# LayerNorm in four blocks of 258 tokens, and the second pointwise convolution by column groups and token quarters

## The chip, the cores and the metric

The kernel runs on one core of a Trainium2 chip. Five engines work side by side: TensorE (PE in the profile; its weight loads are PEld), VectorE (DVE), ScalarE (ACT), GpSimd (POOL) and SyncE (SP), whose queue issues most of the DMAs. Each engine executes its own instructions in order and waits for the others at semaphores. The metric is the device time of one execution in microseconds; lower is better.

## The reference

One inference step of a two-layer trunk over 1024 prompt tokens and 8 decode tokens (T = 1032 columns in the kernel, 1024 features as 8 tiles of 128 partitions). Layer 0 mixes tokens with a Conformer convolution module, layer 1 with a Mamba-2 mixer; each layer then has a SwiGLU feed-forward and a gated per-layer embedding. The change lies in layer 0:

```python
def conformer_mixer(u, buf, w_pw1, b_pw1, w_dw, b_dw, ln_g, ln_b, w_pw2, b_pw2):
    a = u @ w_pw1 + b_pw1
    v = jax.nn.glu(a, axis=-1)
    c, new_buf = causal_dwconv(v, buf, w_dw, b_dw)
    c = jax.nn.silu(layernorm(c, ln_g, ln_b))
    return c @ w_pw2 + b_pw2, new_buf

h = h + o                                          # o is the mixer's result
h = h + swiglu(rmsnorm(h, g_ffn[i]), ...)
```

The layernorm's mean and variance run over the 1024 features of one token, so over the partitions of all 8 tiles.

## The kernel before, in words

Tokens lie along the free dimension. Every big product is done in three passes of a split operand (`mm3`: high times high, high times low, low times high), so each operand, weight or activation, is first split: a copy rounded to the short form (`split`, on ACT, line 110) and the remainder by a subtraction (line 111, on DVE). One 128 x 1024 weight tile is loaded by SP into `wraw` (two buffers) and split into `whi` and `wlo` (`slab`, line 124). One group of the second pointwise convolution (`product`) is 24 matmuls, 8 feature tiles times 3 passes, into one of 7 PSUM banks.

The order of the work around the change:

1. The depthwise convolution ends with `h[m]` (8 tiles of 128 x 1032) and their sum `cs`, which DVE adds up in the three blocks of `BLK` (344 tokens each).
2. While that goes on, PE has filler work: 12 steps of `ple_products` (the projection of the per-layer embeddings, line 240 evicts them), handed out by `FILL` at fixed places of the program.
3. LayerNorm in three blocks of 344 tokens. `center` subtracts the mean (a matmul of `cs` with a constant matrix, line 726; the subtraction, line 732, is on DVE). `square` sums squares into a statistics tile: in block 0 the squares are on ACT (line 194) and the sums on DVE (line 195), in blocks 1 and 2 both are on POOL (lines 186, 188, 195). `finish` is a matmul (line 204), a square root on ACT (line 209, with a table load), a reciprocal on DVE (line 210), and a one-element Silu that brings back the other table (line 742). `apply` multiplies by the reciprocal root (DVE, line 748), does Silu with scale and bias (ACT, line 750), and makes both parts of the split on DVE (lines 751 and 752).
4. After all three blocks `hp.close()` gives up the memory of `h`, and an `Entry` takes it. Only then are the residual's pieces of `x` loaded into its tiles `ha` and `hb` (line 786). `h` here means both halves of 516 tokens, `j` = 0 and 1.
5. The second pointwise convolution for `j`, for `m`, for two quarters `b` of 258 tokens: product, eviction with bias and residual (DVE, line 794), then `Entry.add`: a store to `h_d` in DRAM (line 270), the square (ACT, lines 275 and 278) and its sum (POOL, line 279). All 8 weight tiles are loaded and split twice, once for each half.
6. After `m` = 1 of half 1, `entry.finish(0)` and `entry.prepare(0)`: the RMSNorm of half 0 (line 285 is its matmul), and the operands of the feed-forward (`b1`, `b2`, `t2`, seven split operands). `gate_up` follows with half 0 first, and makes `finish(1)` and `prepare(1)` after its first weights.

The program is written in this order, and a scheduler orders the instructions of each engine by it and by when it expects operands; the SP queue is one of the queues that it orders. Tiles that take memory from a closed pool wait for the last use of each tile that lay there.

Of the kernel before, what the change touches and what calls it, by code (L numbers as in the profile page):

```python
# [16 lines left out]
P = 128  # L17
# [10 lines left out]
BLK = ((0, 344), (344, 344), (688, 344))  # L28
BLKP = ((0, 388), (388, 386), (774, 258))
# [28 lines left out]
def trunk_kernel(ctx: ExitStack, tc: tile.TileContext, I, O):  # L58
# [28 lines left out]
    V.memset(warm, 1.0)  # L87
    half = const.tile([P, 4], F32, name="half")
# [160 lines left out]
    class Entry:  # L249
# [15 lines left out]
        def add(self, j, m, b):  # L265
# [5 lines left out]
            if self.acc[j] is None:  # L271
                self.acc[j] = self.np.tile([P, HT], F32, name="acc", tag="acc")
                self.rstd[j] = self.np.tile([P, HT], F32, name="rstd", tag="rstd", bufs=2)
            if m == 0:
                S.activation(out=self.acc[j][:, o:o + QT], in_=x, func=AF.Square)
                return
            sq = self.np.tile([P, QT], F32, name="sq", tag="sq", bufs=2)
            S.activation(out=sq, in_=x, func=AF.Square)
            G.tensor_tensor(out=self.acc[j][:, o:o + QT], in0=self.acc[j][:, o:o + QT], in1=sq, op=ALU.add)

        def finish(self, j):
            for b in range(2):
# [256 lines left out]
    with tc.tile_pool(name="l0", bufs=2, reuse_waits="tile") as pool:  # L539
# [50 lines left out]
        with tc.tile_pool(name="conv", bufs=2, reuse_waits="tile") as cp:  # L590
# [24 lines left out]
            def conv(m, v):  # L615
# [14 lines left out]
                elif m == KT - 1:  # L630
                    for o, n in BLK:
                        V.tensor_tensor(out=cs[:, o:o + n], in0=cs[:, o:o + n], in1=c[:, o:o + n], op=ALU.add)
                else:
                    V.tensor_tensor(out=cs, in0=cs, in1=c, op=ALU.add)
# [47 lines left out]

            vs = []
# [19 lines left out]
            for m in range(KT):  # L703
# [4 lines left out]
                if m == KT - 1:  # L708
# [4 lines left out]
                    it = chain(ple_products(cp, ps, 1, U[6:], "v"), ple_products(cp, ps, 0, U[4:6], "v", (1,)))  # L713
# [5 lines left out]

            ln = Norm(ps)  # L720
            for _ in range(FILL[1]):
                next(it)
            mus = []
            for o, n in BLK:
                mu = ps.tile([P, 512], F32, name="mu", tag="mm")
                TE.matmul(mu[:, :n], lhsT=mean, rhs=cs[:, o:o + n], start=True, stop=True)
                mus.append(mu)

            def center(b, m):
                o, n = BLK[b]  # L730
                cx = h[m][:, o:o + n]
                return V.tensor_tensor(out=cx, in0=cx, in1=mus[b][:, :n], op=ALU.subtract)

            def square(b, m):
                o, n = BLK[b]
                return ln.add(h[m][:, o:o + n], o, n, V if b == 0 else G, None if b == 0 else G)

            def finish(b, root_behind=(), recip_behind=()):
                root, recip = ln.finish(*BLK[b])
                behind(root, *root_behind)  # L740
                behind(recip, *recip_behind)
                behind(S.activation(out=warm[:, :1], in_=warm[:, 1:], func=AF.Silu), root)
                return root, recip

            def apply(b, m):
                o, n = BLK[b]
                t = npool[0].tile([P, 384], F32, name="un", tag="un", bufs=2)
                x = V.tensor_tensor(out=t[:, :n], in0=h[m][:, o:o + n], in1=ln.rstd[:, o:o + n], op=ALU.mult)
                s = pool.tile([P, 384], F32, name="s", tag="s")
                y = S.activation(out=s[:, :n], in_=t[:, :n], func=AF.Silu, bias=col("ln_b", m), scale=col("ln_g", m))  # L750
                V.tensor_copy(out=U[m][0][:, o:o + n], in_=s[:, :n])  # L751
                z = V.tensor_tensor(out=U[m][1][:, o:o + n], in0=s[:, :n], in1=as32(U[m][0][:, o:o + n]), op=ALU.subtract)  # L752
                return x, y, z

            for m in range(KT):
                center(0, m)
                x = square(0, m)
            for m in range(4):
                behind(center(1, m), x)
                square(1, m)  # L760
            for _ in range(FILL[2]):
                next(it)
            root, recip = finish(0)
            for _ in it:
                pass
            for m in range(KT):
                x, y, z = apply(0, m)
            for m in range(4, KT):
                behind(center(1, m), recip)
                square(1, m)  # L770
            for m in range(KT):
                behind(center(2, m), x)
                square(2, m)
            for b in (1, 2):
                finish(b, (y,), (z,))
                for m in range(KT):
                    x, y, z = apply(b, m)
# [4 lines left out]
    for j in range(2):  # L782
        for b in range(2):
            for m in range(KT):
                o = QT * b
                nc.sync.dma_start(out=entry.h[j][m][:, o:o + QT], in_=I["x"][m, :, HT * j + o:HT * j + o + QT])
        for m in range(KT):
            w = kview(slab(I["w_pw2"][m], 1024), KT)
            for b in range(2):
                o = QT * b  # L790
                a = ps.tile([P, 512], F32, name="a", tag="mm")
                product(a[:, :QT], w, 0, U, HT * j + o, QT)
                hx = entry.h[j][m][:, o:o + QT]
                V.scalar_tensor_tensor(out=hx, in0=a[:, :QT], scalar=col("b_pw2", m), in1=hx, op0=ALU.add, op1=ALU.add)
                entry.add(j, m, b)
            if j == 1 and m == 1:
                entry.finish(0)
# [663 lines left out]
```

## Time and profile before

| | |
|---|---|
| median of 3 runs | 3101.6 us (3101.09 to 3102.29) |
| time of the profiled execution | 3103.0 us |
| its span, first to last instruction | 3101.2 us |
| mean granted TensorE clock | 0.975 of full speed |
| PE busy / DVE busy / ACT busy / POOL busy | 95% / 65% / 45% / 18% of the span |
| depthwise convolution's sum `cs` complete | 266.3 us into the span |
| last matmul of the second pointwise convolution | starts at 417.5 us |

The stage of the change is about 150 us long and lies between 265 and 418 us. Shares over the whole span say nothing about it, so the rows below are taken from windows inside it. "Busy" of a group of rows counts overlapping instructions once; the mean is that of one instruction alone, so busy divided by the count is the pitch of a back-to-back series and the mean is what one costs by itself.

### The profile page before, as it was taken

What the parts mean: (1) busy time and instruction counts of PE and PEld (TensorE: products, weight loads), DVE (VectorE), ACT (ScalarE), POOL (GpSimd) and SP (SyncE); (2) the same over time, 40 slices, a digit from 0 to 9 for tenths busy, and PEclk for the clock granted to TensorE, in tenths of its full rate; (3) what the DMA queues carried; (4) which work ended last, traced back from release to release, by engine and by line L of the source; (5) the groups of instructions that cost most, each with busy time, mean ns of one, the idle gap of its engine ahead of it and who ended that gap; (6) DMA issues with size and microseconds to landing.
All of it is one profiled execution on the core that took longest, in us unless ns stands there. A gap on an engine that the chain in (4) does not pass through costs nothing. (4 is left out here: it accounts for less than half of the span.)

```text
span 3101.2 us, 51140 instructions
## 1 busy us (share of the span) xinstructions
PE 2941.5 (95%) x20513; PEld 2893.8 (93%) x20513; DVE 2022.4 (65%) x3255; ACT 1402.5 (45%) x2470; POOL 556.8 (18%) x571
## 2 busy tenths in 40 slices
PE   9997989999999999999999999988979999989997
PEld 9997889999999999899999999888979999989997
DVE  8778695555444488467788777875595555444486
ACT  6225453333321155667667676732353333321164
POOL 0003210000000021144454444441210000000022
PEclk9998999999999999999999999998999999999998
DMA  6335522222252233122233222442422222252222
GB/s 191 75 80 179 160 88 94 76 79 73 82 185 89 65 111 102 54 87 91 92 108 106 94 92 100 144 159 79 124 77 82 81 83 83 69 179 88 65 88 87
DMA packets 146415, 313.23 MB, mean 101 GB/s; under 512 B 16513, under 2 KB 66049, under 8 KB 146177
## 3 DMA queue, kind: packets, MB, share of 16 engines
q1 hardware_dynamic: 143872, 301.51, 30.0%
q10 hardware_dynamic: 2304, 8.46, 0.7%
q8 instruction: 161, 2.64, 0.4%
q14 instruction: 78, 0.63, 0.1%
HBM read 233.15 MB, written 68.35 MB: 97 GB/s over the span
## 5 line engine op out<-in xcount | busy, mean ns | idle before, releaser
L130 PE MATMUL mm<-u,whi 128*128 128x388 f32 (+3 forms) x1472 | 481.1, 328 | 35.0 <-ACT raw L848 25.2
L131 PE MATMUL mm<-u,whi 128*128 128x388 f32 (+3 forms) x1472 | 487.3, 331 | 7.6 <-DVE u L111 7.6
L132 PE MATMUL mm<-u,wlo 128*128 128x388 f32 (+3 forms) x1472 | 477.7, 325 | 0.6 <-DVE wlo L111 0.6
L110 ACT ACTIVATE whi<-wraw 128x1024 fp32r<-128x1024 f32 (+1 forms) x199 | 207.8, 1044 | 454.4 <-PE a L131 263.7
L130 PEld LDWEIGHTS mm<-u,whi 128*128 128x128 f32 x1472 | 283.3, 193 | 39.2 <-ACT raw L848 26.6
L130 PE MATMUL a<-hh,whi 128*128 128x344 f32 x984 | 309.0, 321 | 10.9 <-ACT hh L110 10.9
L131 PE MATMUL a<-hh,whi 128*128 128x344 f32 x984 | 315.3, 321 | 0.6 <-DVE hh L111 0.6
L132 PE MATMUL a<-hh,wlo 128*128 128x344 f32 x984 | 314.5, 320 | 0.0
L195 POOL TENSOR_TENSOR stat<-stat,sq 128x344 f32<-128x344 f32 x56 | 60.0, 1072 | 1392.7 <-ACT sq L194 1390.4
L131 PEld LDWEIGHTS mm<-u,whi 128*128 128x128 f32 x1472 | 283.9, 193 | 12.4 <-DVE u L111 10.3
L132 PEld LDWEIGHTS mm<-u,wlo 128*128 128x128 f32 x1472 | 283.6, 193 | 2.5 <-DVE wlo L111 0.8
L111 DVE TENSOR_TENSOR wlo<-wraw,whi 128x1024 fp32r<-128x1024 f32 (+1 forms) x199 | 244.3, 1228 | 62.5 <-ACT whi L110 59.2
L460 DVE TENSOR_TENSOR h<-a,h 128x344 f32<-128x344 f32 x288 | 144.7, 512 | 174.9 <-PE a L132 174.1
L130 PE MATMUL a<-u,whi 128*128 128x344 f32 (+1 forms) x712 | 224.9, 317 | 15.4 <-DVE u L751 9.8
L131 PE MATMUL a<-u,whi 128*128 128x344 f32 (+1 forms) x712 | 223.2, 315 | 7.2 <-DVE u L752 7.2
L132 PE MATMUL a<-u,wlo 128*128 128x344 f32 (+1 forms) x712 | 220.9, 313 | 2.7 <-DVE wlo L111 2.7
L130 PEld LDWEIGHTS a<-hh,whi 128*128 128x128 f32 x984 | 184.4, 189 | 11.4 <-ACT hh L110 11.4
L131 PEld LDWEIGHTS a<-hh,whi 128*128 128x128 f32 x984 | 185.5, 189 | 1.0 <-DVE hh L111 1.0
L132 PEld LDWEIGHTS a<-hh,wlo 128*128 128x128 f32 x984 | 185.4, 189 | 0.0
L130 PEld LDWEIGHTS a<-u,whi 128*128 128x128 f32 x712 | 137.3, 193 | 18.3 <-DVE u L751 10.9
L111 DVE TENSOR_TENSOR wal<-sa,wah 128x1024 fp32r<-128x1024 f32 x44 | 53.9, 1224 | 151.6 <-ACT wah L110 151.6
L131 PEld LDWEIGHTS a<-u,whi 128*128 128x128 f32 x712 | 137.1, 193 | 10.0 <-DVE u L752 8.7
(361 smaller groups left out, 8652.6 us busy)
## 6 DMA issues: line engine op xcount, KB each, us to landing
wraw<-in_w_in SPq DMA_DIRECT2D x48, 512.0 KB, 3.7
hid<-hid SPq DMA_DIRECT2D x88, 258.0 KB, 2.5
hraw<-hid SPq DMA_DIRECT2D x44, 516.0 KB, 4.2
wraw<-in_w_gate SPq DMA_DIRECT2D x44, 512.0 KB, 3.2
wraw<-in_w_up SPq DMA_DIRECT2D x44, 512.0 KB, 3.3
wraw<-in_w_pw SPq DMA_DIRECT2D x32, 512.0 KB, 3.4
wraw<-in_w_down SPq DMA_DIRECT2D x32, 512.0 KB, 3.4
am<-ac_d SPq DMA_DIRECT2D x64, 256.0 KB, 3.3
```

What stands on the lines that cost most here:

```text
L110: S.activation(out=hi, in_=raw, func=AF.Copy)
L111: eng.tensor_tensor(out=lo, in0=raw, in1=as32(hi), op=ALU.subtract)
L130: TE.matmul(out, lhsT=wh, rhs=xh, start=start, stop=False, skip_group_check=onto)
L131: TE.matmul(out, lhsT=wh, rhs=xl, start=False, stop=False, skip_group_check=onto)
L132: TE.matmul(out, lhsT=wl, rhs=xh, start=False, stop=stop, skip_group_check=onto)
L195: return eng.tensor_tensor(out=self.acc[:, o:o + n], in0=self.acc[:, o:o + n], in1=sq[:, :n], op=ALU.add)
L460: V.tensor_tensor(out=h[m][:, o:o + n], in0=a[:, :n], in1=h[m][:, o:o + n], op=ALU.add)
```

## The change

- LayerNorm goes by `BLQ`, four blocks of 258 tokens, in place of three of 344. All squares are on ACT, all sums of squares on POOL. The high part of the split is an ACT copy (`split`) in place of a DVE cast.
- The second pointwise convolution of half 0 is in the LayerNorm's part of the program (`pw2_first`): after block 0 the output tiles 0 to 5 for quarter 0, after block 1 the same tiles for quarter 1, with their six split weights kept in memory, and then tiles 6 and 7 for both quarters ahead of `apply(3)`. Its residual is loaded from `x` into a small tile `rx` of its own (4 buffers), the result goes from there to `h_d` in DRAM and is squared into `acc0`, a constant tile.
- After `hp.close()` half 0 is read back from `h_d` into the `Entry`'s tiles, half 1's residual comes from `x` in whole halves (8 loads in place of 16 for each half), and half 1 is computed as before, with its 8 weight tiles loaded again.
- The convolution's pool is closed before the LayerNorm. A new pool `lnw` takes its place, with the filler's staging tiles, the small tiles and four more pairs of split weights.

```diff
+BLQ = tuple((T // 4 * b, T // 4) for b in range(4))
...
+    acc0 = const.tile([P, HT], F32, name="acc0")
...
-                self.rstd[j] = self.np.tile([P, HT], F32, name="rstd", tag="rstd", bufs=2)
+            self.square(self.acc[j][:, o:o + QT], x, m, self.np)
+
+        @staticmethod
+        def square(acc, x, m, pool):
             if m == 0:
-                S.activation(out=self.acc[j][:, o:o + QT], in_=x, func=AF.Square)
+                S.activation(out=acc, in_=x, func=AF.Square)
                 return
-            sq = self.np.tile([P, QT], F32, name="sq", tag="sq", bufs=2)
+            sq = pool.tile([P, QT], F32, name="sq", tag="sq", bufs=2)
             S.activation(out=sq, in_=x, func=AF.Square)
-            G.tensor_tensor(out=self.acc[j][:, o:o + QT], in0=self.acc[j][:, o:o + QT], in1=sq, op=ALU.add)
+            G.tensor_tensor(out=acc, in0=acc, in1=sq, op=ALU.add)

         def finish(self, j):
+            self.rstd[j] = self.np.tile([P, HT], F32, name="rstd", tag="rstd", bufs=2)
...
-                    for o, n in BLK:
+                    for o, n in BLQ:
                         V.tensor_tensor(out=cs[:, o:o + n], in0=cs[:, o:o + n], in1=c[:, o:o + n], op=ALU.add)
...
+        with tc.tile_pool(name="lnw", bufs=1, reuse_waits="tile") as lp:
+            lent.pool = lp
             ln = Norm(ps)
             for _ in range(FILL[1]):
                 next(it)
...
+            def center(b):
+                o, n = BLQ[b]
                 mu = ps.tile([P, 512], F32, name="mu", tag="mm")
                 TE.matmul(mu[:, :n], lhsT=mean, rhs=cs[:, o:o + n], start=True, stop=True)
+                for m in range(KT):
+                    cx = h[m][:, o:o + n]
+                    V.tensor_tensor(out=cx, in0=cx, in1=mu[:, :n], op=ALU.subtract)
+                    ln.add(cx, o, n, G)
+
+            def finish(b):
+                root, recip = ln.finish(*BLQ[b])
                 behind(S.activation(out=warm[:, :1], in_=warm[:, 1:], func=AF.Silu), root)
...
+            def apply(b):
+                o, n = BLQ[b]
+                for m in range(KT):
+                    t = lp.tile([P, QT], F32, name="lt", tag="lt", bufs=4)
+                    V.tensor_tensor(out=t, in0=h[m][:, o:o + n], in1=ln.rstd[:, o:o + n], op=ALU.mult)
+                    S.activation(out=t, in_=t, func=AF.Silu, bias=col("ln_b", m), scale=col("ln_g", m))
+                    split(t, U[m][0][:, o:o + n], U[m][1][:, o:o + n])
+
+            def pw2_first(m, w, b):
+
+                o, n = BLQ[b]
+                x = lp.tile([P, QT], F32, name="rx", tag="rx", bufs=4)
+                nc.sync.dma_start(out=x, in_=I["x"][m, :, o:o + n])
+                a = ps.tile([P, 512], F32, name="a", tag="mm")
+                product(a[:, :n], w, 0, U, o, n)
+                V.scalar_tensor_tensor(out=x, in0=a[:, :n], scalar=col("b_pw2", m), in1=x, op0=ALU.add, op1=ALU.add)
+                nc.sync.dma_start(out=h_d[0][m, :, o:o + n], in_=x)
+                Entry.square(acc0[:, o:o + n], x, m, lp)
+
+            def pw2_weights(m, extra):
+                return kview(slab(I["w_pw2"][m], 1024, lp if extra else None, 4), KT)
+
+            center(0)
+            for _ in range(2):
                 next(it)
+            center(1)
+            finish(0)
             for _ in it:
                 pass
+            ws = [pw2_weights(m, False) for m in range(2)]
+            apply(0)
+            for m in range(6):
+                if m >= 2:
+                    ws.append(pw2_weights(m, True))
+                pw2_first(m, ws[m], 0)
+            finish(1)
+            apply(1)
+            center(2)
+            for m in range(6):
+                pw2_first(m, ws[m], 1)
+            finish(2)
+            center(3)
+            apply(2)
+            finish(3)
+            for m in (6, 7):
+                w = pw2_weights(m, False)
+                for b in range(2):
+                    pw2_first(m, w, b)
+            apply(3)

     hp.close()
     xs = ExitStack()
     entry = Entry(0, ps, xs.enter_context(tc.tile_pool(name="xe0", bufs=1, reuse_waits="tile")))
+    entry.acc[0] = acc0
+    for m in range(KT):
+        nc.sync.dma_start(out=entry.h[0][m], in_=h_d[0][m, :, :HT])
+    for m in range(KT):
+        nc.sync.dma_start(out=entry.h[1][m], in_=I["x"][m, :, HT:])
+    for m in range(KT):
+        w = kview(slab(I["w_pw2"][m], 1024), KT)
...
```

## Rows read from the trace of the kernel before

**Rows 1.** The page's engines: busy us, share of the span, instructions.
```profile
PE 2941.5 (95%) x20513; PEld 2893.8 (93%) x20513; DVE 2022.4 (65%) x3255; ACT 1402.5 (45%) x2470; POOL 556.8 (18%) x571
```
**Rows 2.** Busy time by stage: stretch, length, engines, PE clock, DMA share, GB/s.
```profile
284.80:311.50 26.70, 9.72 (x30) 6.52 (x28) 26.56 (x40) 11.86 (x18) 20.48 (x23) 0.59 0.16 60
311.50:337.00 25.50, 21.14 (x146) 20.12 (x146) 23.57 (x49) 15.18 (x21) 0.74 (x1) 0.90 0.21 66
337.00:345.00 8.00, 6.72 (x35) 6.72 (x36) 4.00 (x9) 3.36 (x8) 2.08 (x3) 0.57 0.97 292
345.00:378.80 33.80, 33.38 (x279) 33.18 (x278) 12.16 (x17) 9.37 (x16) 10.43 (x11) 1.00 0.75 221
378.80:417.60 38.80, 36.48 (x295) 35.67 (x294) 36.64 (x40) 20.96 (x30) 12.95 (x12) 1.00 0.34 108
417.60:455.00 37.40, 30.52 (x209) 28.00 (x208) 35.55 (x44) 21.95 (x32) 2.64 (x2) 0.91 0.15 48
```
**Rows 3.** PE's waits from 284 to 418 us: total us, times, longest us.
```profile
PE a L130 <- DVE u L751: 9.8, 3, 5.0
PE a L131 <- DVE u L752: 7.2, 5, 3.4
PE a L130 <- DVE ha L794: 4.4, 1, 4.4
```
**Rows 4.** PE's timeline: start us, us, engine, line, out<-in, idle before.
```profile
279.35 0.74 PE L204 MATMUL st<-stat,mean 128*128 128x344 f32 x2
...
284.81 0.31 PE L132 MATMUL a<-u,wlo 128*128 128x344 f32 x1
...
378.96 0.60 PE L285 MATMUL st<-acc,mean 128*128 128x258 f32 x2
```
**Rows 5.** DVE's groups from 265 to 337 us: busy us, mean ns | idle before.
```profile
L748 DVE TENSOR_TENSOR un<-h,stat 128x344 f32<-128x344 f32 x24 | 16.2, 690 | 0.1
L752 DVE TENSOR_TENSOR u<-s,u 128x344 fp32r<-128x344 f32 x24 | 14.4, 605 | 0.2
L732 DVE TENSOR_TENSOR h<-h,mu 128x344 f32<-128x344 f32 x24 | 10.5, 504 | 0.1
L751 DVE CAST u<-s 128x344 fp32r<-128x344 f32 x24 | 9.9, 414 | 0.8 <-ACT s L750 0.7
```
**Rows 6.** ACT's groups from 265 to 337 us.
```profile
L750 ACT ACTIVATE s<-un,vec 128x344 f32<-128x344 f32 x24 | 16.0, 672 | 24.0 <-DVE u L752 20.0 <-DVE un L748 3.8
L240 ACT ACTIVATE pstg<-a 128x344 f32<-128x344 f32 x19 | 8.3, 456 | 4.1 <-PE a L132 4.1
L209 ACT ACT_TABLE_LOAD x3 | 3.8, 1283 | 0.4 <-ACT pstg L240 0.4
L209 ACT ACTIVATE stat<-st,eps 128x344 f32<-128x344 f32 x3 | 1.6, 549 | 0.0
```
**Rows 7.** Groups from 337 to 418 us, on DVE, ACT and POOL.
```profile
L111 DVE TENSOR_TENSOR wlo<-wraw,whi 128x1024 fp32r<-128x1024 f32 x12 | 15.7, 1309 | 8.4 <-ACT whi L110 8.0 <-DMA ha<-in_x 0.4
...
L794 DVE SCALAR_TENSOR_TENSOR ha<-a,vec,ha 128x258 f32<-128x258 f32 x16 | 7.5, 484 | 13.1 <-PE a L132 9.5 <-DMA ha<-in_x 2.9 <-DMA hb<-in_x 0.7
...
L288 DVE RECIPROCAL rstd<-rstd 128x258 f32<-128x258 f32 x2 | 3.5, 1766 | 1.0 <-ACT rstd L287 1.0
...
L110 ACT ACTIVATE whi<-wraw 128x1024 fp32r<-128x1024 f32 x12 | 12.7, 1058 | 16.8 <-PE a L131 13.6 <-DMA wraw<-in_w_pw 3.2
L278 ACT ACTIVATE sq<-ha 128x258 f32<-128x258 f32 x14 | 5.6, 413 | 10.4 <-DVE ha L794 9.2 <-POOL acc L279 1.2
...
L279 POOL TENSOR_TENSOR acc<-acc,sq 128x258 f32<-128x258 f32 x26 | 25.5, 990 | 79.2 <-ACT sq L278 66.7 <-ACT acc L275 12.5
```
**Rows 8.** The SP queue's timeline from 261 to 345 us.
```profile
263.74 70.51 SPq L124 DMA_DIRECT2D wraw<-in_w_pw  x6
334.29 7.67 SPq L786 DMA_DIRECT2D ha<-in_x  x16
```
**Rows 9.** The SP queue's waits from 265 to 420 us.
```profile
SPq L124 <- DVE wlo L111: 73.1, 8, 36.0
```

More of the change, by code (lines that the diff above doesn't have):

```diff
@@ L681, in bands, with tile @@
                 V.tensor_tensor(out=phases(c)[0], in0=phases(c)[0], in1=back, op=ALU.add)
+            class Lent:
+                pool = cp
+                def tile(self, *args, **kw):
+                    return self.pool.tile(*args, **kw)
+            lent = Lent()
             vs = []
@@ L712, in trunk_kernel @@
                     U[:4] = [(utile(0), utile(0)) for _ in range(4)]
-                    it = chain(ple_products(cp, ps, 1, U[6:], "v"), ple_products(cp, ps, 0, U[4:6], "v", (1,)))
+                    it = chain(ple_products(lent, ps, 1, U[6:], "v"), ple_products(lent, ps, 0, U[4:6], "v", (1,)))
                     for _ in range(FILL[0]):
@@ L722, in trunk_kernel @@
                 next(it)
-            mus = []
-            for o, n in BLK:
+            def center(b):
+                o, n = BLQ[b]
                 mu = ps.tile([P, 512], F32, name="mu", tag="mm")
                 TE.matmul(mu[:, :n], lhsT=mean, rhs=cs[:, o:o + n], start=True, stop=True)
[L727 to L741, printed above, removed]
-                behind(S.activation(out=warm[:, :1], in_=warm[:, 1:], func=AF.Silu), root)
[L743 to L761, printed above, removed]
+                for m in range(KT):
[4 more added lines that the diff above has]
+                root, recip = ln.finish(*BLQ[b])
+                behind(S.activation(out=warm[:, :1], in_=warm[:, 1:], func=AF.Silu), root)
@@ L762, in trunk_kernel @@
+            def pw2_weights(m, extra):
+                return kview(slab(I["w_pw2"][m], 1024, lp if extra else None, 4), KT)
+            center(0)
+            for _ in range(2):
                 next(it)
-            root, recip = finish(0)
+            center(1)
+            finish(0)
             for _ in it:
                 pass
[L766 to L777, printed above, removed]
+            ws = [pw2_weights(m, False) for m in range(2)]
[5 more added lines that the diff above has]
+            finish(1)
@@ L781, in trunk_kernel @@
     entry = Entry(0, ps, xs.enter_context(tc.tile_pool(name="xe0", bufs=1, reuse_waits="tile")))
-    for j in range(2):
-        for b in range(2):
[L784 to L797, printed above, removed]
-                entry.prepare(0)
-                entry.first.close()
+    entry.acc[0] = acc0
[5 more added lines that the diff above has]
+        w = kview(slab(I["w_pw2"][m], 1024), KT)
+        for b in range(2):
+            o = QT * b
+            a = ps.tile([P, 512], F32, name="a", tag="mm")
+            product(a[:, :QT], w, 0, U, HT + o, QT)
+            hx = entry.h[1][m][:, o:o + QT]
+            V.scalar_tensor_tensor(out=hx, in0=a[:, :QT], scalar=col("b_pw2", m), in1=hx, op0=ALU.add, op1=ALU.add)
+            entry.add(1, m, b)
+        if m == 1:
+            entry.finish(0)
+            entry.prepare(0)
+            entry.first.close()
     h, hp, U, rstd = ffn(0, entry, ps, xs)
```

## The prediction

> **What bounds the kernel now.** I read the page's engine shares first, then PE's busy time by stage, then PE's waits in the stage that the change touches, then the groups of the engines that PE waits for there, and the SP queue last. (The page's chain of waits holds only the last few microseconds of the program and says nothing here.) PE is busy 95% of the span [rows 1], so a step is worth what PE loses beside it. PE ends its filler at 284.81 + 0.31 = 285.1 us [rows 4] and works without a gap until then. In the next 26.7 us it is busy 9.7 us at a granted clock of 0.59, while DVE is busy 26.56 of 26.70 us [rows 2]: DVE sets the pace. PE's waits name it: 9.8 us for the cast and 7.2 us for the remainder of the LayerNorm's operands, the longest 5.0 us, the first wait after the filler [rows 3]. ACT waits 20.0 us for DVE in the same stage [rows 6], and DVE itself has next to no idle time in it [rows 5]. A last wait of 4.4 us is for the residual [rows 3]: SP issues it from 334.29 us on [rows 8], when the memory of `h` is given up; the 8 us after that run at a clock of 0.57 [rows 2]. From 345 us on PE is busy 33.4 of 33.8 us at full clock, and that bound is PE's own.
>
> How much is lost: at full clock 279 matmuls take 33.38 us [rows 2], 0.1196 us each, so a group of 24 takes 2.87 us. Between 285.1 us and the statistics matmul of half 0 at 378.96 us [rows 4] PE has 20 groups to do (16 of half 0, and `m` = 0 and 1 of half 1), 57.4 us, and some 3 us of statistics matmuls at 0.6 to 0.74 us. It takes 93.9 us: 33.5 us are lost. From there to the first feed-forward matmul PE is busy 36.5 of 38.8 us [rows 2].
>
> **The change, part by part.** All ends are compared at that statistics matmul, because what follows it (12 groups, the operands of half 0) has the same instructions before and after.
>
> *Start of block 0.* In the program the matmul of `finish(0)` moves from behind 10 of 12 filler steps to behind 8. Before, it ran at 279.35 us [rows 4], two steps, 5.75 us, ahead of the filler's end at 285.1 us, so PE's order held and not the wait. Now four steps lie behind it, so it comes at about 273.6 us, and POOL's 7 sums, from about 268 us on at 0.75 to 0.99 us [rows 7], end at 273 to 275 us. Root and table load (1.28 + 0.55 us [rows 6]), reciprocal (1.77 us [rows 7]) and three short steps put the first operand at about 280 us, beside the filler; before it came 5 us after it. Block 0 as a whole is done near 289 us by ACT's work, so PE still loses 2 to 3 us at the start.
>
> *PE's bound.* With operands always there: 285.1 + 57.4 + 3 = 345.5 us, a gain of 33.5 us. What remains to be asked is when the last `apply` ends.
>
> *DVE.* It loses 24 casts and 7 sums of squares and gains one reciprocal. Its instructions become 96 of 258 columns: 32 each of center, multiply and remainder. The center's pitch is 10.5 / 24 = 0.44 us at 344 columns [rows 5], so 0.33 us at three quarters is the lower end (an estimate by columns), and three quarters of the means 0.504, 0.690 and 0.605 us the upper: 32 to 43 us in all. With 4 reciprocals (7.1), 8 weight remainders (10.5) and 16 evictions (7.7) [rows 7] that is 57 to 68 us; from 266 us on it ends at 323 to 334 us.
>
> *ACT.* All squares and the high parts of the split are now its own: 32 squares, 32 copies and 16 squares of `pw2_first` at 0.413 us [rows 7] (the copy is taken at the square's price, same shape) 33.0; 32 Silu at 0.50 to 0.67, taken as 0.60 (672 ns at 344 columns [rows 6]) 19.2; 8 weight copies 8.5; four pairs of table loads with a root, 4 x (2 x 1.283 + 0.549) = 12.5; the rest of the filler's evictions 8.3 [rows 6]. Sum 81.5 us: from 266 us on it ends at 347.5 us if nothing overlaps. Series overlap: DVE's center costs 0.504 us alone and 0.44 in series, 13% less [rows 5]; by that ACT ends at 337 us. ACT is then the latest engine, and I take the middle, 342 us. The fourth block's two loads and root are in this sum, 3.1 us.
>
> The Trainium skill speaks against them: its page ScalarE: Activation LUTs, section What ACT_TABLE_LOAD costs, gives about 1283 ns for the load and about 1380 ns for a drain, 2.66 us a switch. The load's mean here is 1283 ns; of the drain the idle ahead of three loads shows 0.4 us in all [rows 6]. By the page eight switches would be 11 us longer.
>
> *Sum.* After the last `apply`, 4 groups of half 1 (11.5 us) stand before the statistics matmul: 342 + 11.5 = 353.5 us against 378.96, a gain of 25 us; 20 with 347.5, 30 with 337.
>
> *What is moved past the queues.* SP: 16 loads of the residual, 0.5 us of issue each (7.67 / 16 [rows 8]), and 16 stores move into the LayerNorm, where SP spends 70.5 us on 6 issues [rows 8]; hidden. Each store waits for its eviction, and the weights are queued behind it; the weights for half 0 have two raw buffers and are wanted every 2.87 us only in quarter 0, after that not for 17 us. New are 8 loads that read half 0 back, 2.1 MB, 7.3 us at the 292 GB/s of the stretch after 337 us [rows 2], ahead of the 8 of half 1's residual, another 7.3 us. They start when `apply(3)` has read `h`. PE's cover is seven PSUM banks, 7 x 2.87 = 20 us, against 15 us; hidden, at 4.4 us and some 3 us of half clock if not (the price of the residual's wait now [rows 2, 3]). Weight splits are 16 as before. The closing of the convolution's pool makes filler and LayerNorm tiles wait for its tiles: nothing, since a staging tile had to wait for them already; up to 5 us if the filler is held.
>
> *Behind the statistics matmul* 0; between 0 and -9 us (the 2.3 and 6.9 us that PE is idle there [rows 2]) if half 1 and the feed-forward's start go more smoothly.
>
> So 3103.0 - 25 = 3078 against the profiled execution; the median of the runs is 1.4 us below that execution, which makes 3077.
>
> **The rivals.** *PE never waits* (15%): ACT's series overlap more, and quarter 2 of half 1 covers the end of `apply(3)`. 33.5 us: 3068, and 3061 with most of the smoother start behind. For it: ACT was idle 24 us for DVE [rows 6], so its true speed was not tested. Against it: the sum of ACT.
>
> *ACT behind POOL* (13%): the squares have two buffers, and each waits for POOL's sum two before it. POOL's sum took 0.99 us on the mean against 0.413 for the square [rows 7]; 5 of each block's squares then hold ACT 0.58 us longer, 11.5 us in four blocks. 347.5 + 11.5 + 11.5 = 370.5 us: gain 8.5, 3093. The drains above would do the same.
>
> The Trainium skill has a rule that would do more: in SBUF — State Buffer, section Who interferes with whom, it says that a DVE instruction with two SBUF inputs and a GpSimd one that reads SBUF exclude each other for the whole instruction. The rows show less: beside 21 us of POOL [rows 2] the multiply and the remainder are 24 x 0.186 + 24 x 0.101 = 6.9 us dearer than the center, which reads one of its inputs from PSUM [rows 5]. As a mechanism of this kernel, 42 sums of 0.99 us that shut DVE out entirely give 57 + 42 = 99 us, 365 + 11.5 = 376.5 us: gain 2.5 us, 3099 (part of the next 5%).
>
> *It doesn't come about* (5%): the scheduler's order, or tiles of the new pool that wait for the convolution's, keep PE's first groups where they are: 3097 to 3103.
>
> *Slower* (7%): half 0 comes back from DRAM late. Its loads stand in SP's order behind weight loads, and SP has waited 73.1 us for DVE's weight remainders, once 36.0 us [rows 9]. If the read-back ends later than the 34 us of PE work behind the statistics matmul, the operands of half 0, a chain in which DVE is busy 36.6 us [rows 2], lie bare. The feed-forward's first units can run beside the last third of it; 25 us and some 7 of half clock stay: 3077 + 32 = 3109. It decides if the last of the 8 loads lands more than about 35 us after `apply(3)`. Against it: PE was busy 6.72 of the 8 us after 337 us [rows 2], so the residual's loads landed soon after their issue from 334.29 us on [rows 8].
>
> **How the numbers follow.** The forecast (25 us gained, own range 3066 to 3087) has 60%; the rivals 15, 13, 5 and 7%. The range 3061 to 3100 holds all but the slower case and some of the one that doesn't come about, and allows for the unknown order of the engines' queues. A measurement of this kernel tells 0.2%, 6 us, from no change: faster than that 0.86, within it 0.07, slower 0.07.
>
> **What would show it.** Right: the first group of the second pointwise convolution starts at 285 to 287 us; PE's waits between 285 us and the statistics matmul fall from 21 to some 9 us and name ACT; ACT is busy over 80% from 266 to 340 us; that matmul comes at 349 to 359 us; no wait for the residual. Wrong: PE still waits for DVE first, the clock stays near 0.6 for more than 10 us, POOL's sums have ACT behind them, or PE stands idle at the feed-forward's start for half 0's operands.

## The result and the profile after

The changed kernel takes 3078.56 us (median of 4 runs, 3073.95 to 3081.57) against 3101.35 us (4 runs, 3100.21 to 3102.29): ratio 0.9926, 95% interval 0.9911 to 0.9941. It is 22.8 us faster; 3077 was forecast. The profiled execution took 3081.57 us, its span is 3079.8 us. So the time was right. The way to it was not: the stage of the change gave 14 to 18 us in place of 25, and the rest came from behind it.

The page's engines, as in [rows 1]:
```profile
PE 2935.8 (95%) x20517; PEld 2891.5 (94%) x20517; DVE 2007.2 (65%) x3250; ACT 1420.7 (46%) x2538; POOL 549.5 (18%) x569
```
Busy time by stage in the kernel after, cut where its own stages end (filler; block 0 to 2; last `apply`; rest of half 1), columns as in [rows 2]:
```profile
285.30:309.00 23.70, 17.36 (x103) 15.97 (x104) 17.01 (x32) 22.43 (x44) 0.86 (x1) 0.78 0.52 178
309.00:348.70 39.70, 37.77 (x308) 37.16 (x306) 28.82 (x57) 26.00 (x57) 21.27 (x28) 1.00 0.46 135
348.70:368.20 19.50, 15.69 (x98) 14.57 (x99) 15.11 (x29) 15.34 (x32) 1.91 (x2) 0.82 0.59 204
368.20:403.60 35.40, 33.62 (x280) 33.21 (x279) 32.34 (x38) 16.89 (x24) 13.76 (x10) 1.00 0.51 164
```
At 0.1196 us for a matmul [rows 2], 103 matmuls are 12.3 us of PE's 23.70, so 11.4 us are lost at the start; in the other three stretches it is 2.9, 7.8 and 1.9. That is 24 us. The same count for the kernel before, over the stretches of [rows 2] from 284.80 to 417.60 us, is 132.8 - 785 x 0.1196 = 38.9 us; 15 us are won. The first feed-forward matmul moves from 417.6 to 403.6 us.

PE's waits of the kernel after from 285 to 404 us, as in [rows 3]:
```profile
PE a L132 <- ACT u L112: 4.5, 2, 2.7
PE a L134 <- DVE wlo L113: 2.4, 3, 1.0
PE st L291 <- ACT stat L211: 1.9, 1, 1.9
PE a L132 <- ACT whi L112: 1.9, 3, 1.2
PE a L132 <- ACT xhi L112: 1.8, 1, 1.8
```
With two smaller ones (1.0 us for POOL's sums, 0.3 for `xlo`) they are 13.8 us. DVE's cast and remainder, 17.0 us of [rows 3], are gone, ACT is named in their place (10.1 us), and the wait for the residual is gone. PE's timeline at the start, as in [rows 4]:
```profile
278.56 0.60 PE L206 MATMUL st<-stat,mean 128*128 128x258 f32 x2
...
284.81 0.32 PE L133 MATMUL a<-u,whi 128*128 128x344 f32 x1
286.33 0.70 PE L206 MATMUL st<-stat,mean 128*128 128x258 f32 x2 [1.05 <-POOL stat L197]
289.69 0.58 PE L132 MATMUL a<-u,whi 128*128 128x258 f32 x1 [2.66 <-ACT u L112]
```
Block 0's statistics matmul runs only 0.8 us earlier than in [rows 4], where 273.6 us was foretold, and the first group still starts 4.6 us behind the filler's end at 285.1 us. ACT's timeline says why (start, us):
```profile
278.42 0.44 ACT L242 ACTIVATE pstg<-a 128x344 f32<-128x344 f32 x1
278.76 0.41 ACT L196 ACTIVATE sq<-h 128x258 f32<-128x258 f32 x1
...
281.34 1.28 ACT L211 ACT_TABLE_LOAD   x1
282.64 0.48 ACT L211 ACTIVATE stat<-st,eps 128x258 f32<-128x258 f32 x1
...
285.78 1.05 ACT L112 ACTIVATE xhi<-wraw 128x1024 fp32r<-128x1024 f32 x1
286.73 0.80 ACT L242 ACTIVATE pstg<-a 128x344 f32<-128x344 f32 x2
287.40 0.61 ACT L756 ACTIVATE lt<-lt,vec 128x258 f32<-128x258 f32 x1
...
289.22 0.42 ACT L112 ACTIVATE u<-lt 128x258 fp32r<-128x258 f32 x1
```
Between the matmul and the root ACT still has squares of block 1 and the filler's evictions to do; between the reciprocal and the first Silu come evictions and a weight copy.

The second place is the middle. ACT is busy 11.64 of 24.00 us from 309 to 333 us, the stretch in which it was to be the pacer. The kernel after there, first POOL and PE, then ACT, then the stretch:
```profile
323.31 1.49 POOL L197 TENSOR_TENSOR stat<-stat,sq 128x258 f32<-128x258 f32 x1 [0.20 <-ACT sq L196]
```
```profile
331.98 0.60 PE L206 MATMUL st<-stat,mean 128*128 128x258 f32 x2
332.42 0.60 PE L741 MATMUL mu<-cs,mean 128*128 128x258 f32 x2
345.19 0.60 PE L206 MATMUL st<-stat,mean 128*128 128x258 f32 x2
```
```profile
330.32 1.28 ACT L211 ACT_TABLE_LOAD   x1
332.62 0.48 ACT L211 ACTIVATE stat<-st,eps 128x258 f32<-128x258 f32 x1 [1.02 <-PE st L206]
```
```profile
309.00:333.00 24.00, 24.00 (x198) 23.83 (x197) 13.87 (x28) 11.64 (x26) 12.96 (x16) 1.00 0.52 151
```
POOL's sums of block 2 end at 324.8 us, but their matmul stands in PE's order behind the groups of quarter 1 and runs at 331.98, and block 3's mean right behind it. PE is never idle here, so no wait names the fault; it is a queue's order. The last copy of `apply(3)` ends at 361.0 us, where 342 was forecast.

The groups of DVE and ACT from 265 to 361 us, as in [rows 5, 6]:
```profile
L755 DVE TENSOR_TENSOR lt<-h,stat 128x258 f32<-128x258 f32 x32 | 14.7, 497 | 0.2
L113 DVE TENSOR_TENSOR u<-lt,u 128x258 fp32r<-128x258 f32 x31 | 13.8, 475 | 4.9 <-ACT u L112 4.9
L744 DVE TENSOR_TENSOR h<-h,mu 128x258 f32<-128x258 f32 x32 | 11.0, 415 | 5.6 <-PE mu L741 5.6
```
```profile
L756 ACT ACTIVATE lt<-lt,vec 128x258 f32<-128x258 f32 x32 | 18.1, 594 | 2.8 <-DVE lt L755 2.7
L112 ACT ACTIVATE u<-lt 128x258 fp32r<-128x258 f32 x32 | 12.1, 407 | 0.1
L196 ACT ACTIVATE sq<-h 128x258 f32<-128x258 f32 x28 | 11.5, 413 | 3.3 <-POOL stat L197 2.9 <-DVE h L744 0.3
```

### The profile page after: what moved, and what is told of

It is laid out like the page before. It is cut to its first block, busy times and chain, and to the rows that moved or that the text cites. A ratio compares the mean times of both kernels' runs of the same rounds, so it can differ in the third digit from the quotient of the medians.

```text
span 3079.8 us, 51237 instructions
## 1 busy us (share of the span) xinstructions
PE 2935.8 (95%) x20517; PEld 2891.5 (94%) x20517; DVE 2007.2 (65%) x3250; ACT 1420.7 (46%) x2538; POOL 549.5 (18%) x569
## 5 line engine op out<-in xcount | busy, mean ns | idle before, releaser
L197 POOL TENSOR_TENSOR stat<-stat,sq 128x344 f32<-128x344 f32 (+1 forms) x70 | 68.1, 974 | 1452.7 <-ACT sq L196 1449.9
L113 DVE TENSOR_TENSOR wlo<-wraw,whi 128x1024 fp32r<-128x1024 f32 (+1 forms) x195 | 238.0, 1221 | 56.7 <-ACT whi L112 55.3
L132 PE MATMUL a<-u,whi 128*128 128x344 f32 (+1 forms) x648 | 204.4, 317 | 6.7 <-ACT u L112 4.5
L133 PE MATMUL a<-u,whi 128*128 128x344 f32 (+1 forms) x648 | 203.6, 315 | 0.1
L134 PE MATMUL a<-u,wlo 128*128 128x344 f32 (+1 forms) x648 | 201.3, 313 | 2.4 <-DVE wlo L113 2.4
L132 PEld LDWEIGHTS a<-u,whi 128*128 128x128 f32 x648 | 123.6, 191 | 8.9 <-ACT u L112 5.1
L134 PEld LDWEIGHTS a<-u,wlo 128*128 128x128 f32 x648 | 123.4, 191 | 3.5 <-DVE wlo L113 3.0
```

The lines of the kernel that those rows point to most:

```text
L113: eng.tensor_tensor(out=lo, in0=raw, in1=as32(hi), op=ALU.subtract)
L132: TE.matmul(out, lhsT=wh, rhs=xh, start=start, stop=False, skip_group_check=onto)
L133: TE.matmul(out, lhsT=wh, rhs=xl, start=False, stop=False, skip_group_check=onto)
L134: TE.matmul(out, lhsT=wl, rhs=xh, start=False, stop=stop, skip_group_check=onto)
L197: return eng.tensor_tensor(out=self.acc[:, o:o + n], in0=self.acc[:, o:o + n], in1=sq[:, :n], op=ALU.add)
```

## The experiments

Each time is a median beside runs of the kernel before on the same chip. "ff" is the start of the first feed-forward matmul; in every run all groups of the second pointwise convolution stand ahead of it. "center to ff" is the time to it from the start of block 0's center matmul, with which the stage begins. "ys" are the first matmul with `btok` in layer 1's state-space stage, and the time from it to the last. All four are from one profiled execution.

| run | us | ratio to before, 95% | ff | center to ff | first ys | ys, length |
|---|---|---|---|---|---|---|
| before | 3101.35 | | 417.6 | 152.1 | 1339.1 | 807.9 |
| after | 3078.56 | 0.9926 (0.9911-0.9941) | 403.6 | 136.8 | 1320.8 | 804.2 |
| e0_control | 3076.55 | 0.9912 (0.9898-0.9925) | 399.9 | 135.7 | 1316.3 | 801.1 |
| e1_cast | 3081.39 | 0.9931 (0.9917-0.9945) | 398.2 | 133.5 | 1316.9 | 808.6 |
| e2_order | 3077.30 | 0.9914 (0.9901-0.9928) | 398.6 | 134.3 | 1319.1 | 804.2 |
| e7_cast_order | 3084.28 | 0.9933 (0.9920-0.9947) | 403.1 | 137.0 | 1321.4 | 810.0 |
| e8_one_copy | 3083.45 | 0.9939 (0.9927-0.9952) | 402.4 | 137.6 | 1320.9 | 806.6 |
| e4_ln4 | 3093.72 | 0.9968 (0.9956-0.9979) | 415.0 | 148.7 | 1335.1 | 803.3 |
| e5_nogroups | 3088.61 | 0.9955 (0.9943-0.9968) | 411.6 | 146.3 | 1332.0 | 804.3 |
| e6_readback | 3085.76 | 0.9947 (0.9934-0.9959) | 405.9 | 139.4 | 1328.4 | 803.6 |
| e9_before_m0 | 3097.72 | 0.9983 (0.9974-0.9992) | 419.6 | 155.3 | 1340.3 | 803.7 |
| e12_written_earlier | 3073.58 | 0.9903 (0.9888-0.9919) | 400.2 | 135.1 | 1317.7 | 787.6 |
| e13_early_stat | 3080.02 | 0.9925 (0.9913-0.9937) | 402.7 | 137.3 | 1320.0 | 804.7 |
| e14_late_residual | 3078.26 | 0.9918 (0.9904-0.9931) | 399.2 | 132.0 | 1318.6 | 805.1 |

**The kernel after again** shows how far one execution tells: its `ff` is 3.7 us earlier than in the first profile, of which 2.5 us stand already at block 0's statistics matmul (276.1 against 278.6 us). Differences of `ff` alone under some 4 us are not told apart. The stage itself began at another time (center matmul at 266.82 and 264.21 us); counted from there the two executions are 1.1 us apart, and the change is worth 15.3 and 16.4 us.

> The changed kernel itself, once more. In its first profile the feed-forward's first matmul (pA) came 14.1 us earlier than before (403.6 against 417.6 us) and the end 21.4 us earlier, so about 7 us came from behind the changed stage, mostly in layer 1. Theory A (a property of the program: other orders of DVE, ACT, POOL and SP behind the stage): again 403 to 405 us for pA and 6 to 8 us from behind it. Theory B (chance of one execution): pA within 1 us of 403.6, and the share behind the stage anywhere from 2 to 10 us. Time 3074 to 3082 under both.

Both theories missed: `ff` moved by 3.7 us, and 11.0 us come from behind it, against 7.4 in the first pair of profiles.

**ACT at the start: the copy on DVE, and the root's place.** Two single edits.
```diff
-split(t, U[m][0][:, o:o + n], U[m][1][:, o:o + n])
+V.tensor_copy(out=U[m][0][:, o:o + n], in_=t)                       # e1
+V.tensor_tensor(out=U[m][1][:, o:o + n], in0=t, in1=as32(...), op=ALU.subtract)
...
+behind(root, *last)        # e2: last = the last ACT copy of the apply before
```


> One edit on the changed kernel: the high part of the split in apply is a DVE cast again, and not an ACT copy. ACT loses 32 copies, 13 us at 0.41 us, DVE gains 32 casts at about 0.31 us, 10 us. Theory ACT (ACT paces the LayerNorm's stage; it was busy 22.4 of 23.7 us from 285 to 309 us): pA 4 to 6 us earlier than in the changed kernel, 398 to 400 us, time about 3074. Rival DVE (DVE with POOL paces it, as before the change): no gain or up to 4 us later, 3078 to 3083.

> One edit on the changed kernel: the root of each block, with its two table loads, is queued on ACT behind the last copy of the block before it. In the changed kernel block 1's pair of loads (3.3 us) stands in the middle of block 0's Silu while PE waits. Theory ACT: the first groups of the second pointwise convolution come out 2 to 3 us earlier, pA at 400 to 402 us, time about 3076. Rival (the next block's operands become late instead): PE waits at the start of quarter 1, pA at 404 to 408 us, time 3079 to 3083.

From 285 to 309 us PE is busy 20.93 us in e1 and 20.81 us in e2 (next two fences), against 17.65 and 18.68 us in the two executions of the kernel after. So ACT's load and the table pair in the middle of block 0's Silu each cost some 2 to 3 us there. The whole time gains nothing that can be told from the control; both also have another order in layer 1 (below).
```profile
285.00:309.00 24.00, 20.93 (x141) 19.68 (x140) 21.91 (x49) 18.18 (x33) 2.31 (x3) 0.86 0.58 188
```
```profile
285.00:309.00 24.00, 20.81 (x149) 19.88 (x150) 17.93 (x33) 20.52 (x43) 1.44 (x2) 0.86 0.58 188
```
Both together:

> The edits of the two kernels with the DVE cast and with the ordered roots together, on the changed kernel. Each alone brought the feed-forward's first matmul (pA) to 398.2 and 398.6 us, against 399.9 and 403.6 in two profiles of the changed kernel. Theory ACT: they act on the same engine and add up in part, pA 394 to 397 us. Rival (what is left is DVE's and POOL's): 398 to 399 us. Behind the stage PE's order from layer 1 on is that of the kernel before, matmul for matmul, as with the cast alone; if that order costs 4 to 8 us (2680 us from pA to the end with it, 2673 to 2676 with the others), the time is 3077 to 3080 in spite of the earlier pA.

They don't add up: `ff` is 403.1 us, 137.0 us behind the center's matmul. In e7 from 340 to 370 us it is DVE that is busy, 27.84 of 30.00 us, at a granted clock of 0.83, and PE's longest waits from 285 to 400 us are DVE's: 3.8 us for the operands' remainder and 3.8 for the weights'. That DVE's load is what keeps them from adding up is not shown by a run of its own:
```profile
340.00:370.00 30.00, 22.90 (x145) 20.08 (x144) 27.84 (x57) 17.33 (x29) 7.82 (x8) 0.83 0.60 198
```

**What each half of the change is worth.** e4 keeps only the four blocks: the groups on half 0, the residual tile of their own and the read-back are as before. e5 keeps the residual's way, but writes half 0's groups behind all of LayerNorm, tile by tile.
```diff
-for m in range(6):                     # e5, and the same for quarter 1
-    pw2_first(m, ws[m], 0)
...
-for m in (6, 7):
+apply(3)
+for m in range(KT):
     w = pw2_weights(m, False)
```


> Part of the change alone: LayerNorm in four blocks with its new engines, but the second pointwise convolution of half 0 after it, with the Entry's residual loads and no read-back, as in the kernel before. Theory of the prediction (the gain is from PE having the first quarters to do during the LayerNorm, and from the residual of half 0 not waiting for the memory of h): most of the gain is gone, 3093 to 3101, with a wait of PE for the residual again. Rival (the gain is from the shorter blocks and DVE's lighter load): 3080 to 3088.

> The changed kernel, with the second pointwise convolution of half 0 written behind all of the LayerNorm, tile by tile with both quarters and its weights loaded one by one, still with its own residual tile and the read-back. Theory (PE gains by whole column groups on quarters that are ready): PE starves again from 285 to 320 us, only the residual's wait stays away: pA 406 to 412 us, 3083 to 3090. Rival (the four blocks, the residual's own tile and the scheduler are enough): pA 400 to 404 us, 3075 to 3080.

In e4 PE is busy 7.76 us from 285 to 309 us, and `ff` comes at 415.0 us; e5 is at 411.6. By `ff` the four blocks alone bring 2.6 us of the stage's 14 to 18, the order by column groups and quarters 8 to 12 (3.4 and 9.5 to 10.6 counted from the center's matmul). Between e4 and e5 lie 2 to 3 us for the residual's tile and the read-back, which no run tests alone; the wait for the residual that e4's expectation foretold is not there, 0.5 us of PE's waits stand at `ha`. In whole time e4 and e5 are 10.0 and 14.9 us faster than the kernel before on the same chip, since behind `ff` they gain 8.0 and 7.9 us, as the kernel after gains 7.4.
```profile
285.00:309.00 24.00, 7.76 (x27) 5.63 (x27) 18.19 (x34) 21.38 (x47) 9.63 (x13) 0.71 0.23 84
```

**The statistics matmuls of blocks 2 and 3.** e13 forces them ahead of half of quarter 1's groups; e12 only moves lines of the program.
```diff
 for m in range(3):                     # e12 (with finish(0) ahead of center(1)); e13 adds behind(matmul, st(2), mu(3)) in m = 3 to 5
     pw2_first(m, ws[m], 1)
 finish(2)
 center(3)
+for m in range(3, 6):
+    pw2_first(m, ws[m], 1)
```


> The kernel after, with one change in PE's queue: the groups of column groups 3 to 5 on quarter 1 are queued behind the statistics matmul of block 2 and the center's matmul of block 3, so that these two run some 15 us earlier in PE's order instead of behind all of quarter 1. Theory (ScalarE stands idle from 309 to 333 us because those matmuls stand behind PE's groups): ACT's idle time in 309:333 falls from 12 us to under 7, the last u copy ends at 350 us or earlier instead of 360.6, the first feed-forward matmul comes at 392 to 397 us (after 400 to 404), and the kernel takes 3068 to 3073 us. Rival (the earlier statistics matmul only moves the gap: VectorE, or PE that now waits for POOL's sums in front of its groups, is the next bound): PE loses at 309:340 what it saves later, first feed-forward matmul at 399 to 404 us, 3075 to 3081 us.

> The kernel after with two lines of the program moved and nothing forced: finish(0) is written before center(1), and finish(2) and center(3) after three instead of six groups of quarter 1. The statistics matmuls of blocks 2 and 3 come 7 and 11 us earlier in PE's order. Theory (they hold ScalarE): about half of what the forced order gives: first feed-forward matmul at 396 to 400 us, 3071 to 3076 us. Rival (the order is not what holds ScalarE): 400 to 404 us, 3076 to 3081 us. Layer 1 has an order of its own here, which by the runs so far is one of the shorter ones (2672 to 2677 us behind the first feed-forward matmul).

PE's timeline in e12, to be read against 331.98 and 345.19 us above:
```profile
323.80 0.70 PE L206 MATMUL st<-stat,mean 128*128 128x258 f32 x2 [0.33 <-POOL stat L197]
...
333.25 0.70 PE L206 MATMUL st<-stat,mean 128*128 128x258 f32 x2 [0.23 <-POOL stat L197]
```
ACT's idle time from 309 to 340 us falls from 13.7 us (11.7 in the control) to 8.1 in e12 and 8.5 in e13, and the last copy ends at 351.9 and 353.1 us, against 361.0 (357.6). So the cause of ACT's idleness was right, and ACT's end came 4.5 to 9 us earlier. But `ff` is 400.2 and 402.7 us, 135.1 and 137.3 us behind the center's matmul: the gain is given back. Where, e12 shows: the stretch in which PE stands, and ACT's line in it.
```profile
365.00:375.00 10.00, 5.93 (x36) 5.52 (x35) 9.91 (x13) 4.53 (x6) 4.21 (x1) 0.83 0.60 206
```
```profile
367.44 1.06 ACT L112 ACTIVATE whi<-wraw 128x1024 fp32r<-128x1024 f32 x1 [5.97 <-DMA wraw<-in_w_pw]
```
The SP queue of e12 has all 16 loads of half 0 and half 1 ahead of the weights of column groups 2 and 3:
```profile
349.94 4.15 SPq L810 DMA_DIRECT2D hb<-in_x  x8
354.13 5.21 SPq L808 DMA_DIRECT2D ha<-h_d  x8
359.75 1.00 SPq L272 DMA_DIRECT2D h_d<-hb  x2
361.11 0.33 SPq L126 DMA_DIRECT2D wraw<-in_w_pw  x1
```
e12's median is the lowest of all, 3073.58 us; its interval overlaps that of the kernel after, so it is not shown to be the better kernel. Its layer 1 has an order of its own: `ys` is some 16 us shorter and the time behind it some 15 us longer.

**The loads ahead of the weights.** e12, with five of half 1's eight loads each behind a weight load:
```diff
-for m in range(KT):
+for m in range(3):
     nc.sync.dma_start(out=entry.h[1][m], in_=I["x"][m, :, HT:])
...
     w = kview(slab(I["w_pw2"][m], 1024), KT)
+    if 2 <= m < KT - 1:
+        behind(nc.sync.dma_start(out=entry.h[1][m + 1], in_=...), slab.load)
```


> The kernel e12_written_earlier with the loads of half 1's residual spread out: three are issued at the start of half 1 as before, each of the other five only behind the weight load of the column group before it. In e12 and e13 the two weight loads of column groups 2 and 3 stood behind all 16 residual loads (4.2 MB at about 390 GB/s), ScalarE's weight copy came at 367 to 369 us, and PE lost 3 to 5 us and ran at half clock at 365 to 375 us. Theory (those transfers are what took back the gain of the earlier statistics matmuls): weights land 3 to 5 us earlier, PE's wait for the weight copy at 362 to 372 us falls below 1.5 us, and the first feed-forward matmul comes at 394 to 398 us (e12 400.2, e13 402.7). Rival (the stage is bound there by VectorE, which makes half 0's operands and is busy 25 of 30 us): the waits change their name, the first feed-forward matmul stays at 399 to 404 us. Behind it PE's order in layer 1 is, but for 8 matmuls, that of the kernel before, so by the runs so far what follows takes 2678 to 2684 us, 5 us more than in e12, and not 2672 to 2677: 3072 to 3082 us in all with the theory, 3077 to 3088 with the rival.

The weight copy that came at 367.44 us comes at 363.44, PE's wait for it is gone, and PE is busy 9.58 in place of 5.93 of the 10 us, at full clock. Yet `ff` is 399.2 us, over the 394 to 398 of the theory. This execution began late, though: from the center's matmul it is 132.0 us, 3.1 us less than e12 and 3.7 to 4.8 less than the two executions of the kernel after. So the loads took that much of the gain, as far as one execution tells. The rival's DVE, which makes half 0's operands, is indeed busy 29.48 of the 30 us behind it (25.21 in e12), but PE does 234 matmuls there, 28.0 us at 0.1196, so at most 2.0 us are lost to DVE; that it holds the end is not shown. The larger loss is still at the start, where 103 matmuls stand in 24 us. The median gains nothing on the control, since this kernel has the order of before in layer 1 (below).
```profile
285.00:309.00 24.00, 17.61 (x103) 15.93 (x102) 17.67 (x33) 23.24 (x47) 0.86 (x1) 0.79 0.53 176
```
```profile
365.00:375.00 10.00, 9.58 (x81) 9.37 (x79) 10.00 (x13) 4.09 (x7) 1.75 (x2) 1.00 0.73 251
```
```profile
370.00:400.00 30.00, 28.11 (x234) 27.70 (x233) 29.48 (x34) 16.18 (x23) 11.84 (x9) 1.00 0.43 145
```

**The read-back's margin.** Half 0 is read back three times in place of once.
```diff
-nc.sync.dma_start(out=entry.h[0][m], in_=h_d[0][m, :, :HT])
+for _ in range(3):
+    nc.sync.dma_start(out=entry.h[0][m], in_=h_d[0][m, :, :HT])
```


> The kernel after, with half 0 of the residual read back from DRAM three times into the same place instead of once: 16 more loads, 4.2 MB more, some 14 to 15 us of transfer at the 292 GB/s of that stretch. Theory (the read-back is hidden behind the groups of half 1 with a margin): the first feed-forward matmul moves by at most 2 us from 400 to 404 us, 3075 to 3082 us. Rival (the read-back stands close to the path, as in the slower case of the prediction): PE waits for half 0's operands at the feed-forward's start or for half 1's residual, the first feed-forward matmul comes 8 to 15 us later, 3085 to 3095 us.

`ff` moves by 2.3 us against the first profile of the kernel after (the start is alike there, 278.3 and 278.6 us), but the median by 7 to 9 us, and the first `ys` by 7.6 us. The time is the rival's, the place only half. DVE, which in the kernel after makes half 0's operands from 370 to 380 us without a gap, is busy 1.94 us there:
```profile
370.00:380.00 10.00, 8.52 (x72) 8.31 (x70) 1.94 (x4) 1.79 (x4) 2.12 (x3) 1.00 1.04 358
380.00:390.00 10.00, 9.27 (x63) 8.97 (x64) 8.65 (x12) 4.06 (x7) 2.29 (x3) 0.83 1.03 387
```
The 4.2 MB more take 11 to 12 us at 358 to 387 GB/s; some 4 of these were covered. DVE's waits there name PE's groups and not the loads (8.3 us and 0.3): the evictions stand ahead of the operands in its order, and whether the loads or that order cost the 7 us was not tested. A single read-back is hidden, with little to spare.

**The time behind the stage.** By the lines and tiles of PE's rows, the two kernels' orders differ at 520 of the last 11570 matmuls (layer 1), though no line of that layer was changed: the scheduler found another order. Read in the same way, e1, e7, e8 and e14 have the order of before; e0, e5 and e6 that of after, e13 too but for 12 places; e2, e4 and e12 have orders of their own. e9 is the kernel before with one cast in eight moved to ACT, which gives layer 1 the order of after:
```diff
+if m == 0:
+    S.activation(out=U[m][0][:, o:o + n], in_=s[:, :n], func=AF.Copy)
+else:
     V.tensor_copy(out=U[m][0][:, o:o + n], in_=s[:, :n])
```


> The kernel with the DVE cast and the ordered roots, with one high part of 32 (block 3, tile 7) on ACT. The stage is the same but for that one instruction (pA within 1.5 us of that kernel's); the scheduler's order in layer 1 is another. Theory order (the share of the gain behind the stage is the scheduler's order there): the end comes 4 to 8 us earlier than with the DVE cast and the ordered roots alone, 3071 to 3075. Rival (chance, or a cause in the stage): same time within 2 us.

> The kernel before, with the high part of tile 0 of each of its three blocks as an ACT copy in place of a DVE cast: 3 instructions in the changed stage, which keeps its waits (pA 416 to 419 us). PE's order from layer 1 on becomes that of the changed kernel but for 8 of 11570 matmuls. Theory order: 4 to 7 us faster than before, from behind the stage, about 3097. Rival (the share behind the stage comes from the change itself or is chance): 3101 to 3105, as before.

The expectation for e8 rests on a wrong premise: its order is that of e7, matmul for matmul, so its equal time says nothing against the theory. e9 has it the other way: its `ff` is 2 us later than before, and it is faster, ratio 0.9983 (0.9974 to 0.9992), some 5 us. The `ys` stage of the kernel before, then of e9:
```profile
L1109 PE MATMUL ys<-xdd,btok x128: 377/378/634, 1339.1 to 2147.0; 128*128 128x256 f32 x128
```
```profile
L1112 PE MATMUL ys<-xdd,btok x128: 377/378/631, 1340.3 to 2144.0; 128*128 128x256 f32 x128
```
With the order of before the length is 806.6 to 810.0 us (before, e1, e7, e8; mean 808.3). In eight others it is 801.1 to 804.7 (mean 803.6); e14, with 805.1, lies between. The stretch in which the orders part tells them apart better: in the kernel before its first differing matmul runs at 2054.38 us, and from that place in PE's order to the last `ys` matmul it takes 92.6 to 94.5 us in the five runs with the order of before (e14 93.1), and 88.6 to 89.4 us in the five with that of after. The order is worth 4 to 5 us.

## Why the prediction was right in time and wrong in its way

*Right.* DVE set the pace, and the change took it off: no wait for a cast is left in the stage. ACT took its place at the start, as e1 and e2 show. The blocks of DVE cost what the step gave them: 14.7 + 13.8 + 11.0 = 39.5 us, within 32 to 43. ACT's groups lay within 3% of their prices (407 and 413 ns for 0.413 us, 594 for 0.60). The residual's wait went, and in the kernel after no wait of PE names a load or a store. The rival of ACT behind POOL is refuted at its size: 2.9 us of such waits, where it needed 11.5.

*Wrong: the gain of 25 us in the stage.* It was 14.0 us by the first pair of profiles and 17.7 by the control (15.3 and 16.4 counted from the center's matmul). Two terms failed.

The start was to lose 2 to 3 us and lost 11.4. The matmul of `finish(0)` was moved two steps in the program and came 0.8 us earlier (3.3 in the control): the scheduler gave it a place by its own times, and POOL's sums, foretold from 268 us on, began at 270.84 and ended at 276.4 us: ACT's first square ran at 270.03 us, and the squares stand on an ACT that also evicts the filler. Each later step of block 0 then went through the same queue. The step counted the chain's instructions, and not what stands between them on ACT. e1 and e2, which thin that queue in two ways, each give back 2 to 3 us there.

ACT's end was to be 342 us and was 361.0. The sum of its work was right: it was busy 74.8 us from 266 to 360.6 us, within the 71 to 81.5 that the step's two ends give. But the step let ACT work without a gap, and it had nothing to do for half of the stretch from 309 to 333 us, since the operands of the next block hung on matmuls behind PE's groups. e12 and e13 show this by taking it away: 4.5 to 9 us. That this alone brought next to nothing to the end is a point which the prediction missed altogether: once ACT ends earlier, the weights behind 16 loads are next (e12 against e14). In the kernel after itself they are not: SP issues two weight tiles at 341.45 and 348.42 us, ahead of the loads from 356.87 us on, and ACT copies them without waiting for a DMA. The step that called the loads hidden had counted PE's cover in PSUM banks, and not the weights queued behind them. What is next after the loads is not shown.

The comparison at the statistics matmul of half 0 failed too: it runs at 348.69 us, next to the foretold 349 to 359, but at another place, ahead of half 1's groups; the number proves nothing. Of the other signs, the first group starts at 289.69 us and not by 287, PE's waits fall to 13.8 us and not to 9, and ACT is busy 54.89 of 74.00 us from 266 to 340 us, 74% and not over 80; the residual's wait is gone and ACT is named, as foretold.

*What made the total right.* Behind `ff` the first pair of profiles gains 7.4 us more. 4.3 us of it come between `ff` and the first `ys` (921.5 and 917.2 us) and 3.7 us in the `ys` stage; behind that the kernel after is 0.6 us longer. The second is the scheduler's order, which nothing in the prediction foresaw. The first lies within the 0 to 9 us that it allowed for a smoother start of the feed-forward; what made it was not tested, and stays open: the same length is 916.4 to 922.5 us in the other runs, by no rule that they show.

By the Trainium skill (ScalarE: Activation LUTs, What ACT_TABLE_LOAD costs) a switch costs a drain of about 1380 ns beside its load; here the root starts 0.02 us behind a load of 1.28 us, and the engine worked up to the load, so the trace does not show it.

The prediction's reading of POOL and DVE goes by means, and these hide what single rows show. Of the 32 multiplies of the kernel after, 20 that no sum of POOL overlaps took 0.37 to 0.43 us, and the other 12 0.42 to 0.96; 26 remainders without overlap took 0.42 us on the mean, 5 with it 0.75. The center, which reads one input from PSUM, took 0.36 to 0.42 us beside POOL or not. The two engines take turns: two remainders, 1.58 us in place of 0.8, each end some 0.3 us behind a sum that had begun before it, and the sum of 323.31 us above took 1.49 us, because a weight remainder had begun before it.
```profile
322.89 1.30 DVE L113 TENSOR_TENSOR wlo<-wraw,whi 128x1024 fp32r<-128x1024 f32 x1 [1.64 <-ACT whi L112]
343.30 1.58 DVE L113 TENSOR_TENSOR u<-lt,u 128x258 fp32r<-128x258 f32 x2 [0.69 <-ACT u L112]
```
```profile
343.16 0.64 POOL L197 TENSOR_TENSOR stat<-stat,sq 128x258 f32<-128x258 f32 x1
343.76 0.83 POOL L284 TENSOR_TENSOR acc<-acc,sq 128x258 f32<-128x258 f32 x1
```
By the Trainium skill (SBUF — State Buffer, Who interferes with whom) a DVE instruction with two SBUF inputs contends with a GpSimd one that reads SBUF; the trace agrees. It cost these multiplies and remainders some 4 us in all (12 x 0.20 + 5 x 0.33), not the 42 us of the rival, since 23 of POOL's 42 sums ran while DVE did neither of these, and the others overlapped them in part.

## What to carry to other kernels

A sum of an engine's work gives its end only if its operands come in time: look, for each block, which engine's queue holds the matmul that releases it, since an engine that is never idle names no culprit. When one bound is taken away, walk on to the next ones before summing the gain: here ACT's queue, PE's order and the loads ahead of the weights were worth between some 1 and 5 us each, and two fixes of one queue did not add. And with a scheduler in between, measure the part of the program that was not changed as well: 4 to 5 of 22.8 us came from there.

## What was not expected of the hardware

The 16 loads moved at 352 to 398 GB/s in the middle slices of their transfer in the kernel after, above the 292 of [rows 2]; in e12, where weight loads were queued behind them, ACT stood 5.97 us for the weights. A sum of POOL and a DVE instruction with two inputs in SBUF each waited for the other to end, up to some twice their own time, while means over the stage showed a few hundredths of a us. Two profiled executions of the same kernel put the same matmul 3.7 us apart.
